# Attention of the running streams: from split matmuls over the whole array to plain float32 in four column strips

## The chip, the cores and the metric

The kernel runs on one core of a Trainium2 chip. The metric is the device time of one execution in microseconds, as the median of several executions. The kernel before takes 2970.55 us (median of 3, 2970.44 to 2970.97). One execution was taken by the hardware profiler; its own time and its records are what the profile shows.

The engines are TensorE (PE; loads of its stationary operand are listed apart as PEld), VectorE (DVE), ScalarE (ACT), GpSimd (POOL) and SyncE (SP), which here issues nearly all DMAs. Each engine takes its instructions in the order of its own queue.

## The reference, cut to what matters

The program is one inference step of a layer for two groups of requests: a prompt of 1040 positions (16 meta rows and 1024 frames) and eight running streams ("sample") with 16 new frames each. The change touches only the attention of the running streams. For each of the eight streams and 16 heads of width 64, 16 queries look at 272 cached keys and 16 new ones:

```
def stick_breaking(q, k, v, q_pos, k_pos):
    z = einsum('bqhd,bshd->bhqs', q, k) * (SB_HEAD_DIM ** -0.5)
    reach = k_pos[None, :] < q_pos[:, None]
    log_beta = log_sigmoid(z)
    log_keep = where(reach, log_sigmoid(-z), 0.0)
    later = cumsum(log_keep, axis=3, reverse=True) - log_keep
    w = where(reach, exp(log_beta + later), 0.0)
    return einsum('bhqs,bshd->bqhd', w, v)
```

So a weight is the sigmoid of its score times the product of one minus the sigmoids of all later keys. There is no softmax and no sum over rows. All inputs and outputs are float32.

## The kernel before, in words

The layer runs as phases in one program: norm and projections, the state-space part (`phase_ssd`), the prompt's attention (`phase_att`), the running streams' attention (`phase_smp`, which calls `sample_att`), the merge of the branches (`phase_merge`) and the feed-forward part. Big matmuls use a float32r form in which each operand is split into a high and a low part: `split` (L95 to L98) copies the rounded high part on ACT (L97) and subtracts it on DVE (L98), and `mm3` (L109 to L119) adds three products, high by high, high by low, low by high. `weights` (L100 to L107) loads and splits a weight tile in the same way.

`sample_att` works in 16 blocks: eight streams `b`, and in each two halves `hf` of eight heads, that is four pairs `j` of heads, 128 channels each. A block does this:

1. Load 256 cached keys and values of the half (`kt`, `vt`, L861 to L864, 512 KB each, on SP), from a common pool `ck` with four buffers.
2. Transpose the keys, eight 128x128 transposes into two `pk` tiles of PSUM (L135 is the line of every transpose), and split each into `Ksh` and `Ksl` (L97, L98). The last 16 cached keys and the 16 new keys are copied behind them by POOL (L869); the last 16 cached keys of all streams were transposed and split once ahead of the loop (`kch`, `kcl`).
3. Copy the queries, split as well, into `qdh` and `qdl` (L873): for pair `j` a stationary operand of 128 columns in which only columns 32j to 32j+31 are not zero, 16 for each head of the pair.
4. Scores `z`: four pairs times three products accumulate into one PSUM tile of 128 x 288 (L889, L892, L893). As each pair's operand is zero outside its own 32 columns, the sum over pairs puts pair `j` into rows 32j to 32j+31.
5. Weights: sigmoid on ACT (L895), the causal mask of the new keys and one minus it on POOL (L896, L898), a reversed running product on DVE (L899), and two multiplications on DVE (L902, L903).
6. Three transposes of the weights into `wT`, split into `wTh` and `wTl`. The values are split into `Vsh` (ACT, L882) and `Vsl` (POOL and DVE, L884). The last 32 values of four streams share tiles `V3h`, `V3l`, and `w3` holds the weights that belong to them, zero elsewhere.
7. Outputs `o`: three groups of keys times three products, 512 columns each (L912 to L914). Every row of the result holds its own weights against the values of all eight heads; only the diagonal blocks are wanted.
8. Copy the whole 128x512 to `od` (ACT, L916), transpose it in four pieces, and pick the diagonal blocks by two strided copies into `aout` (L924).

Between these blocks the gate projections run as filler. `paced` (L976 to L982) hands out three column tiles of a projection at a time; each is tied by `issue_after` to the first score matmul of a block (`marks`), so it cannot be issued earlier. Of the eight projections left after the prompt's attention six go into this phase, and RESERVE = 2 are kept for the start of the merge. All else about the order is set by a planner that simulates the program and orders each engine's queue by it (`schedule_with_timeline_sim`). A PSUM tile of the phase takes a whole bank: two for the gates, two `pk`, one `z`, two `wT`, one `o`. Pools of SBUF are laid out one behind the other in the order in which `phase_smp` names them, and a tile waits for the earlier users of its memory.

The merge begins with the two reserve gates, while `ssd_operands` (L941 on) loads rows of `s_y` into `yt` (L949), scales them (L951) and splits them (L952, L953).

`sample_state` (L528 on), in the state-space part, already writes plain float32 matmuls into 32-row slices of a PSUM tile (L549).

Of the kernel before, what the change touches and what calls it, by code (L numbers as in the profile page):

```python
# [13 lines left out]
F32 = mybir.dt.float32  # L14
F32R = mybir.dt.float32r
# [8 lines left out]
TP = META + SEQ  # L24
# [53 lines left out]
class Kernel:  # L78
# [738 lines left out]
    def sample_att(self, rate):  # L817
        nc, a, ap, pa = self.nc, self.a, self.ap, self.pa
        marks, done = [], 0
        out = self.tile(ap, [128, 8, TS], F32, 'aout', bufs=1)  # L820
        qs = [self.tile(ap, [128, 8, TS], F32R, n, bufs=1) for n in ('qhs', 'qls')]
        for t, src in zip(qs, (self.s_qh, self.s_ql)):
            nc.sync.dma_start(t.bitcast(F32), src[:, TP - T0:T2].rearrange("(j p) t -> p j t", p=128))

        kc, kn = ([self.tile(ap, [128, 8, TS], F32R, n + x, bufs=1) for x in 'hl'] for n in ('kc', 'kn'))
        for t, src in zip(kn, (self.s_kh, self.s_kl)):
            nc.sync.dma_start(t.bitcast(F32), src[:, TP:T].rearrange("(j p) t -> p j t", p=128))
        for hf in range(2):
            lk = self.tile(ap, [128, 512], F32, 'last', bufs=2)
            nc.sync.dma_start(lk, self.s_ck[:, 512 * hf:512 * hf + 512])  # L830
            pk = self.tile(pa, [128, 512], F32, 'pk', bufs=2)
            for j in range(4):
                self.T_(pk[:, 128 * j:128 * j + 128], lk[:, 128 * j:128 * j + 128])
            self.split(*(t[:, 4 * hf:4 * hf + 4] for t in kc), pk.rearrange("p (j s) -> p j s", j=4))
        qd = [[self.tile(ap, [128, 640], F32R, f'qd{x}{i}', bufs=1) for x in 'hl'] for i in range(2)]
        for i in range(2):
            for x in range(2):
                nc.gpsimd.memset(qd[i][x].bitcast(F32), 0.0)

        w3 = [self.tile(ap, [128, 224], F32, f'w3{hf}', bufs=1) for hf in range(2)]  # L840
        for x in w3:
            nc.gpsimd.memset(x, 0.0)
        for b in range(NB):
            if b % 4 == 0:
                V3 = []
                for hf in range(2):
                    c0 = 512 * hf
                    lv = self.tile(ap, [128, 512], F32, 'last', bufs=2)
                    for i in range(4):
                        cv = a['cache_v'][0, b + i].rearrange("s h d -> s (h d)")  # L850
                        nc.sync.dma_start(lv[32 * i:32 * i + 16], cv[256:272, c0:c0 + 512])
                        t0 = TP + 16 * (b + i)
                        nc.sync.dma_start(lv[32 * i + 16:32 * i + 32].rearrange("t (j c) -> t j c", c=128),
                                          self.s_v[4 * hf:4 * hf + 4, t0:t0 + 16].rearrange("j t c -> t j c"))
                    V3.append([self.tile(ap, [128, 512], F32R, n, bufs=2) for n in ('V3h', 'V3l')])
                    self.split(*V3[hf], lv)
            for hf in range(2):
# [5 lines left out]
                vt = self.tile(self.ckp, [128, 2, 512], F32, 'ck')  # L863
                nc.sync.dma_start(vt, cv[0:256].rearrange("(j p) c -> p j c", p=128))  # L864
                Kh, Kl = (self.tile(ap, [128, 4, 288], F32R, n) for n in ('Ksh', 'Ksl'))
                Q = qd[(2 * b + hf) % 2]
                for x, K in enumerate((Kh, Kl)):
                    for i, k in enumerate((kc, kn)):
                        nc.gpsimd.tensor_copy(K[:, :, 256 + 16 * i:272 + 16 * i],  # L869
                                              k[x][:, 4 * hf:4 * hf + 4, 16 * b:16 * b + 16].bitcast(F32))  # L870
                    for e in range(2):
                        es = slice(64 * e, 64 * e + 64)
                        nc.gpsimd.tensor_copy(Q[x].rearrange("p (j c) -> p j c", c=160)[es, :, 16 * e:16 * e + 16],  # L873
                                              qs[x][es, 4 * hf:4 * hf + 4, 16 * b:16 * b + 16].bitcast(F32))
                for j in range(0, 4, 2):
# [4 lines left out]
                    self.split(Kh[:, j:j + 2, 0:256], Kl[:, j:j + 2, 0:256], pk.rearrange("p (j c) -> p j c", j=2))  # L880
                Vh, Vl = (self.tile(ap, [128, 2, 512], F32R, n) for n in ('Vsh', 'Vsl'))
                nc.scalar.copy(Vh, vt)  # L882
                for i, eng in enumerate((nc.gpsimd, nc.vector)):
                    eng.tensor_tensor(out=Vl[:, i], in0=vt[:, i], in1=Vh[:, i].bitcast(F32), op=ALU.subtract)  # L884
                ps = self.tile(pa, [128, 512], F32, 'z')
                z = ps[:, 0:288]
                for j in range(4):
                    qh, ql = (Q[x][:, 128 * j:128 * j + 128] for x in range(2))
                    mk = nc.tensor.matmul(z, qh, Kh[:, j], start=(j == 0), stop=False)  # L889
                    if j == 0:  # L890
                        marks.append(mk)
                    nc.tensor.matmul(z, qh, Kl[:, j], start=False, stop=False)  # L892
                    nc.tensor.matmul(z, ql, Kh[:, j], start=False, stop=(j == 3))  # L893
# [10 lines left out]
                pt = self.tile(pa, [128, 512], F32, 'wT', bufs=2)  # L904
                for i, x in enumerate((B[:, 0:128], B[:, 128:256], w)):
                    self.T_(pt[:, 128 * i:128 * i + 128], x)
                wh, wl = (self.tile(ap, [128, 3, 128], F32R, n) for n in ('wTh', 'wTl'))
                self.split(wh, wl, pt[:, 0:384].rearrange("p (i c) -> p i c", c=128))
                po = self.tile(pa, [128, 512], F32, 'o')
                vs = [(Vh[:, 0], Vl[:, 0]), (Vh[:, 1], Vl[:, 1]), V3[hf]]  # L910
                for i, (vh, vl) in enumerate(vs):
                    nc.tensor.matmul(po, wh[:, i], vh, start=(i == 0), stop=False)  # L912
                    nc.tensor.matmul(po, wh[:, i], vl, start=False, stop=False)
                    nc.tensor.matmul(po, wl[:, i], vh, start=False, stop=(i == 2))  # L914
# [385 lines left out]
```

## Time and profile before

| what | value |
|---|---|
| median of 3 executions | 2970.55 us (2970.44 to 2970.97) |
| the profiled execution | 2969.59 us |
| its span, first to last instruction | 2967.9 us |
| mean granted TensorE clock | 0.994 |
| TensorE busy | 2909.5 us, 98% |
| first and last score matmul of the running streams (L889, L893) | 1481.5 and 1638.8 us |
| last transposes of `od` | from 1654.4 us |

In the profile a matmul's record runs from its start until its result has landed, so records of matmuls in sequence overlap, and busy time is not occupancy. The distance between starts of matmuls that follow each other without a wait is what one costs. In the views, a row of a timeline has start, duration, engine, line, operation, out<-in, the shape and a count of merged records; in brackets stands the idle time of the engine before it and what ended it. A row of groups has the shape and count, then busy time, mean ns of one, and idle time ahead. A row of a window gives its length and each engine's busy time and instructions, then the granted clock, the DMA engines' busy share and GB/s. A row of waits has total time, times and the longest.

### The profile page before, as it was taken

What the parts mean: (1) busy time and instruction counts of PE and PEld (TensorE: products, weight loads), DVE (VectorE), ACT (ScalarE), POOL (GpSimd) and SP (SyncE); (2) the same over time, 40 slices, a digit from 0 to 9 for tenths busy, and PEclk for the clock granted to TensorE, in tenths of its full rate; (3) what the DMA queues carried; (4) which work ended last, traced back from release to release, by engine and by line L of the source; (5) the groups of instructions that cost most, each with busy time, mean ns of one, the idle gap of its engine ahead of it and who ended that gap; (6) DMA issues with size and microseconds to landing.
All of it is one profiled execution on the core that took longest, in us unless ns stands there. A gap on an engine that the chain in (4) does not pass through costs nothing.

```text
span 2967.9 us, 45503 instructions
## 1 busy us (share of the span) xinstructions
PE 2909.5 (98%) x17399; PEld 2764.3 (93%) x17399; DVE 1711.7 (58%) x2578; ACT 1259.3 (42%) x2611; POOL 626.7 (21%) x1009
## 2 busy tenths in 40 slices
PE   7999999999999999999999999999999999999998
PEld 6998988989889999999899899999999999999998
DVE  6457666676657777777634531446655454545447
ACT  5445454454444455544544310224534242424245
POOL 1024132231322233333333000003201010101013
PEclk9999999999999999999999999999999999999999
DMA  6435355354574555554344642545211111111113
GB/s 196 115 86 159 110 150 149 88 158 118 155 224 136 138 139 145 147 139 106 110 155 132 203 152 87 166 122 170 60 48 44 44 44 37 45 44 44 37 44 121
DMA packets 430826, 338.98 MB, mean 114 GB/s; under 512 B 27264, under 2 KB 406476, under 8 KB 430600
## 3 DMA queue, kind: packets, MB, share of 16 engines
q1 hardware_dynamic: 429103, 333.25, 39.1%
q8 instruction: 137, 2.24, 0.3%
q10 hardware_dynamic: 1504, 2.82, 0.3%
q14 instruction: 82, 0.66, 0.1%
HBM read 244.84 MB, written 91.67 MB: 113 GB/s over the span
## 4 chain that ended last, share of the span: by engine, by line
PE 84%; DMA 5%; DVE 3%; ACT 2%; issue 1%; POOL 1%; SPq 1%; DVEq 0%; ACTq 0%; POOLq 0%
PE mm L115 23%; PE mm L118 22%; PE mm L119 22%; PE wT L135 2%; DMA yt<-s_y 1%; PE yd L501 1%; PE z L732 1%; PE z L735 1%; PE st L484 1%; PE px L135 1%; PE o L759 1%; DMA zf<-s_z 1%; PE o L756 1%; PE yo L510 1%; DMA wf<-in_w_out 1%
## 5 line engine op out<-in xcount | busy, mean ns | idle before, releaser
L115 PE MATMUL mm<-sh,wh 128*128 128x384 f32 (+3 forms) x2520 | 869.2, 346 | 5.0 <-ACT sh L952 1.8
L118 PE MATMUL mm<-sl,wh 128*128 128x384 f32 (+3 forms) x2520 | 868.8, 345 | 3.4 <-DVE sl L98 2.6
L119 PE MATMUL mm<-sh,wl 128*128 128x384 f32 (+3 forms) x2520 | 864.3, 343 | 0.0
L118 PEld LDWEIGHTS mm<-sl,wh 128*128 128x128 f32 (+1 forms) x2520 | 474.9, 188 | 18.7 <-issue 10.3
L115 PEld LDWEIGHTS mm<-sh,wh 128*128 128x128 f32 (+1 forms) x2520 | 474.6, 188 | 16.3 <-issue 5.2
L119 PEld LDWEIGHTS mm<-sh,wl 128*128 128x128 f32 (+1 forms) x2520 | 474.8, 188 | 9.2 <-issue 7.5
L106 DVE TENSOR_TENSOR wl<-wf,wh 128x1024 fp32r<-128x1024 f32 (+2 forms) x205 | 253.3, 1236 | 305.8 <-ACT wh L105 304.7
L118 PE MATMUL mm<-pl,wh 128*128 128x386 f32 x1248 | 424.9, 340 | 0.0
L115 PE MATMUL mm<-ph,wh 128*128 128x386 f32 x1248 | 424.6, 340 | 0.0
L119 PE MATMUL mm<-ph,wl 128*128 128x386 f32 x1248 | 422.8, 339 | 1.2 <-DVE wl L106 1.1
L105 ACT CAST wh<-wf 128x1024 fp32r<-128x1024 f32 (+2 forms) x205 | 212.7, 1038 | 478.3 <-PE mm L118 455.9
L1167 DVE SCALAR_TENSOR_TENSOR acc<-fx,cwf,acc 128x384 f32<-128x384 f32 (+1 forms) x352 | 170.9, 516 | 155.4 <-ACT acc L1165 151.7
L119 PEld LDWEIGHTS mm<-ph,wl 128*128 128x128 f32 x1248 | 236.2, 189 | 2.3 <-DVE wl L106 1.8
L115 PEld LDWEIGHTS mm<-ph,wh 128*128 128x128 f32 x1248 | 236.3, 189 | 0.6
L118 PEld LDWEIGHTS mm<-pl,wh 128*128 128x128 f32 x1248 | 235.2, 188 | 1.7
L699 DVE TENSOR_TENSOR_SCAN keep<-keep 128x144 f32<-128x144 f32 (+7 forms) x128 | 180.1, 1409 | 52.0 <-POOL keep L698 51.3
L115 PE MATMUL mm<-ah,wh 128*128 128x384 f32 x528 | 179.7, 340 | 0.0
L119 PE MATMUL mm<-ah,wl 128*128 128x384 f32 x528 | 179.2, 339 | 0.0
L118 PE MATMUL mm<-al,wh 128*128 128x384 f32 x528 | 178.9, 339 | 0.0
L1094 POOL TENSOR_TENSOR sq<-sq,sq 128x386 f32<-128x386 f32 (+1 forms) x39 | 57.9, 1484 | 446.4 <-ACT sq L1093 438.5
L1192 DVE TENSOR_TENSOR h<-mm,h 128x384 f32<-128x384 f32 x144 | 79.7, 555 | 120.0 <-PE mm L119 119.5
L98 DVE TENSOR_TENSOR wTl<-wT,wTh 128x512 fp32r<-128x512 f32 (+3 forms) x176 | 102.9, 602 | 77.1 <-ACT wTh L97 76.4
(334 smaller groups left out, 4526.0 us busy)
## 6 DMA issues: line engine op xcount, KB each, us to landing
wf<-in_w_in SPq DMA_DIRECT2D x80, 512.0 KB
wf<-in_w_up SPq DMA_DIRECT2D x44, 512.0 KB
t<-s_ac SPq DMA_DIRECT2D x36, 512.0 KB
wf<-in_w_down SPq DMA_DIRECT2D x28, 512.0 KB
wf<-in_w_out SPq DMA_DIRECT2D x24, 512.0 KB
s_y<-x SPq DMA_DIRECT2D x16, 577.0 KB
yt<-s_y SPq DMA_DIRECT2D x16, 577.0 KB
KH<-s_kh SPq DMA_DIRECT2D x32, 260.0 KB
```

The source lines that it names most:

```text
L98: nc.vector.tensor_tensor(out=l, in0=x, in1=h.bitcast(F32), op=ALU.subtract)
L105: nc.scalar.copy(wh, wf)
L106: nc.vector.tensor_tensor(out=wl, in0=wf, in1=wh.bitcast(F32), op=ALU.subtract)
L115: i = nc.tensor.matmul(p, wh[:, k, :], mh[:, c:c + w], start=s, stop=False)
L118: nc.tensor.matmul(p, wh[:, k, :], ml[:, c:c + w], start=False, stop=False)
L119: nc.tensor.matmul(p, wl[:, k, :], mh[:, c:c + w], start=False, stop=e)
L135: self.nc.tensor.transpose(out, in_, self.ident[:k, :k])
L484: first = nc.tensor.matmul(pS, Bt, xe.rearrange("p h d -> p (h d)"), start=True, stop=True)
L699: nc.vector.tensor_tensor_scan(out=K[:, ::-1], data0=K[:, ::-1], data1=K[:, ::-1], initial=1.0, op0=ALU.mult, op1=ALU.min)
L1094: nc.gpsimd.tensor_tensor(out=acc[:, :w], in0=acc[:, :w], in1=sq, op=ALU.add)
L1167: nc.vector.scalar_tensor_tensor(out=op, in0=src(q), scalar=w(q), in1=op, op0=ALU.mult, op1=ALU.add)
L1192: self.nc.vector.tensor_tensor(out=h, in0=p, in1=h, op=ALU.add)
```

## The change

The running streams' attention no longer splits anything. Queries and new keys are put together again from their stored parts (one addition each, DVE and POOL); cached keys, values and weights stay as they are. Each pair of heads gets its own strip of 32 columns of the array: the stationary operand of the scores is 128x32 in place of 128x128, four matmuls write four 32-row slices of `z`, each complete in itself. The outputs are twelve matmuls, three groups of keys for each strip, and each strip multiplies only with its own pair's 128 values, so the result is 128x128 and already holds just the wanted heads (and within a pair both heads' products). It needs one transpose in place of four, into the same bank. The two copies of transposed keys go one to ACT and one to DVE. `V3` is loaded straight into its tile. PSUM: `wT` goes from two banks to one, `o` from one to two. SBUF: `vt` gets its own pool with four buffers in the phase, so that `ck` serves keys alone. Pacing, RESERVE and all else stay. The line numbers below 815 don't change.

```diff
-        qs = [self.tile(ap, [128, 8, TS], F32R, n, bufs=1) for n in ('qhs', 'qls')]
-        for t, src in zip(qs, (self.s_qh, self.s_ql)):
-            nc.sync.dma_start(t.bitcast(F32), src[:, TP - T0:T2].rearrange("(j p) t -> p j t", p=128))
...
+        both = lambda n: [self.tile(ap, [128, 8, TS], F32, n + x, bufs=1) for x in 'hl']
+        qs, kn = both('q'), both('kn')
...
+        for (h, l), eng in ((qs, nc.vector), (kn, nc.gpsimd)):
+            eng.tensor_tensor(out=h, in0=h, in1=l, op=ALU.add)
+        q, kn = qs[0], kn[0]
+        kc = self.tile(ap, [128, 8, TS], F32, 'kc', bufs=1)
...
-            self.split(*(t[:, 4 * hf:4 * hf + 4] for t in kc), pk.rearrange("p (j s) -> p j s", j=4))
+            nc.scalar.copy(kc[:, 4 * hf:4 * hf + 4], pk.rearrange("p (j s) -> p j s", j=4))
+        qd = [self.tile(ap, [128, 4, 32], F32, f'qd{i}', bufs=1) for i in range(2)]
...
-                vt = self.tile(self.ckp, [128, 2, 512], F32, 'ck')
+                vt = self.tile(ap, [128, 2, 512], F32, 'vt', bufs=4)
...
-                    self.split(Kh[:, j:j + 2, 0:256], Kl[:, j:j + 2, 0:256], pk.rearrange("p (j c) -> p j c", j=2))
-                Vh, Vl = (self.tile(ap, [128, 2, 512], F32R, n) for n in ('Vsh', 'Vsl'))
-                nc.scalar.copy(Vh, vt)
-                for i, eng in enumerate((nc.gpsimd, nc.vector)):
-                    eng.tensor_tensor(out=Vl[:, i], in0=vt[:, i], in1=Vh[:, i].bitcast(F32), op=ALU.subtract)
+                    (nc.vector.tensor_copy if j else nc.scalar.copy)(K_[:, j:j + 2, 0:256], pk.rearrange("p (j c) -> p j c", j=2))
...
                 for j in range(4):
-                    qh, ql = (Q[x][:, 128 * j:128 * j + 128] for x in range(2))
-                    mk = nc.tensor.matmul(z, qh, Kh[:, j], start=(j == 0), stop=False)
+                    mk = nc.tensor.matmul(z[32 * j:32 * j + 32], Q[:, j], K_[:, j], start=True, stop=True)
                     if j == 0:
                         marks.append(mk)
-                    nc.tensor.matmul(z, qh, Kl[:, j], start=False, stop=False)
-                    nc.tensor.matmul(z, ql, Kh[:, j], start=False, stop=(j == 3))
...
-                pt = self.tile(pa, [128, 512], F32, 'wT', bufs=2)
+                pt = self.tile(pa, [128, 512], F32, 'wT')
...
-                wh, wl = (self.tile(ap, [128, 3, 128], F32R, n) for n in ('wTh', 'wTl'))
-                self.split(wh, wl, pt[:, 0:384].rearrange("p (i c) -> p i c", c=128))
-                po = self.tile(pa, [128, 512], F32, 'o')
-                vs = [(Vh[:, 0], Vl[:, 0]), (Vh[:, 1], Vl[:, 1]), V3[hf]]
-                for i, (vh, vl) in enumerate(vs):
-                    nc.tensor.matmul(po, wh[:, i], vh, start=(i == 0), stop=False)
-                    nc.tensor.matmul(po, wh[:, i], vl, start=False, stop=False)
-                    nc.tensor.matmul(po, wl[:, i], vh, start=False, stop=(i == 2))
-                od = self.tile(ap, [128, 512], F32, 'od', bufs=1)
-                nc.scalar.copy(od, po)
-                pd = self.tile(pa, [128, 512], F32, 'wT', bufs=2)
-                for j in range(4):
-                    self.T_(pd[:, 128 * j:128 * j + 128], od[:, 128 * j:128 * j + 128])
+                wt = self.tile(ap, [128, 3, 4, 32], F32, 'wt')
+                nc.scalar.copy(wt, pt[:, 0:384].rearrange("p (i j c) -> p i j c", i=3, j=4))
+                po = self.tile(pa, [128, 512], F32, 'o', bufs=2)
+                for i, v in enumerate((vt[:, 0], vt[:, 1], V3[hf])):
+                    for j in range(4):
+                        nc.tensor.matmul(po[32 * j:32 * j + 32, 0:128], wt[:, i, j], v[:, 128 * j:128 * j + 128],
+                                         start=(i == 0), stop=(i == 2))
+                od = self.tile(ap, [128, 128], F32, 'od')
+                nc.scalar.copy(od, po[:, 0:128])
+                self.T_(po[:, 128:256], od)
...
             self.ap = {n: self.pool(c2, "smpa_" + n, 2) for n in (
-                'last', 'qdh0', 'qdl0', 'qdh1', 'qdl1', 'qhs', 'qls', 'knh', 'knl', 'kch', 'kcl', 'Ksh', 'Ksl', 'V3h', 'V3l',
-                'v', 'r', 'newton', 'beta', 'keep', 'Vsh', 'Vsl', 'w30', 'w31', 'wTh', 'wTl', 'od', 'aout')}
+'last', 'qd0', 'qd1', 'w30', 'w31', 'qh', 'ql', 'knh', 'knl', 'kc', 'Ks', 'vt', 'v', 'r', 'newton', 'beta', 'keep',
+                'V3', 'wt', 'od', 'aout')}
```

More of the change, by code (lines that the diff above doesn't have):

```diff
@@ L833, in sample_att @@
                 self.T_(pk[:, 128 * j:128 * j + 128], lk[:, 128 * j:128 * j + 128])
[L834 to L838 removed]
+            nc.scalar.copy(kc[:, 4 * hf:4 * hf + 4], pk.rearrange("p (j s) -> p j s", j=4))
+        qd = [self.tile(ap, [128, 4, 32], F32, f'qd{i}', bufs=1) for i in range(2)]
         w3 = [self.tile(ap, [128, 224], F32, f'w3{hf}', bufs=1) for hf in range(2)]
[L841 removed]
+        for x in qd + w3:
             nc.gpsimd.memset(x, 0.0)
@@ L844, in sample_att @@
             if b % 4 == 0:
-                V3 = []
+                V3 = [self.tile(ap, [128, 512], F32, 'V3', bufs=4) for hf in range(2)]
                 for hf in range(2):
                     c0 = 512 * hf
-                    lv = self.tile(ap, [128, 512], F32, 'last', bufs=2)
                     for i in range(4):
                         cv = a['cache_v'][0, b + i].rearrange("s h d -> s (h d)")
-                        nc.sync.dma_start(lv[32 * i:32 * i + 16], cv[256:272, c0:c0 + 512])
+                        nc.sync.dma_start(V3[hf][32 * i:32 * i + 16], cv[256:272, c0:c0 + 512])
                         t0 = TP + 16 * (b + i)
-                        nc.sync.dma_start(lv[32 * i + 16:32 * i + 32].rearrange("t (j c) -> t j c", c=128),
+                        nc.sync.dma_start(V3[hf][32 * i + 16:32 * i + 32].rearrange("t (j c) -> t j c", c=128),
                                           self.s_v[4 * hf:4 * hf + 4, t0:t0 + 16].rearrange("j t c -> t j c"))
-                    V3.append([self.tile(ap, [128, 512], F32R, n, bufs=2) for n in ('V3h', 'V3l')])
-                    self.split(*V3[hf], lv)
             for hf in range(2):
@@ L862, in sample_att @@
                 nc.sync.dma_start(kt, ck[0:256].rearrange("(j p) c -> p j c", p=128))
-                vt = self.tile(self.ckp, [128, 2, 512], F32, 'ck')
+                vt = self.tile(ap, [128, 2, 512], F32, 'vt', bufs=4)
                 nc.sync.dma_start(vt, cv[0:256].rearrange("(j p) c -> p j c", p=128))
-                Kh, Kl = (self.tile(ap, [128, 4, 288], F32R, n) for n in ('Ksh', 'Ksl'))
+                K_ = self.tile(ap, [128, 4, 288], F32, 'Ks')
                 Q = qd[(2 * b + hf) % 2]
[L867 to L874, printed above, removed]
+                for i, k in enumerate((kc, kn)):
+                    nc.gpsimd.tensor_copy(K_[:, :, 256 + 16 * i:272 + 16 * i], k[:, 4 * hf:4 * hf + 4, 16 * b:16 * b + 16])
+                for e in range(2):
+                    es = slice(64 * e, 64 * e + 64)
+                    nc.gpsimd.tensor_copy(Q[es, :, 16 * e:16 * e + 16], q[es, 4 * hf:4 * hf + 4, 16 * b:16 * b + 16])
                 for j in range(0, 4, 2):
```

11 lines of the change are left out of this document (5 added, 6 removed).

## The prediction

> **What bounds the kernel now.** First the page, the line of busy times and that of what the DMAs moved in each fortieth of the span:
>
> ```profile
> PE 2909.5 (98%) x17399; PEld 2764.3 (93%) x17399; DVE 1711.7 (58%) x2578; ACT 1259.3 (42%) x2611; POOL 626.7 (21%) x1009
> ...
> GB/s 196 115 86 159 110 150 149 88 158 118 155 224 136 138 139 145 147 139 106 110 155 132 203 152 87 166 122 170 60 48 44 44 44 37 45 44 44 37 44 121
> ```
>
> TensorE is busy for 98% of the span, so work taken from it counts, if the stage that it is taken from is bound by it too. The edit lies in `sample_att`, whose instructions stand between 1472 and 1655 us. So, second, the windows over that stretch:
>
> ```profile
> core 0: us, PE busy (x) PEld busy (x) DVE busy (x) ACT busy (x) POOL busy (x), PEclk, DMA share, GB/s
> 1472.00:1482.00 10.00, 5.13 (x27) 4.09 (x28) 6.00 (x9) 5.82 (x9) 9.51 (x23) 0.73 0.55 154
> 1482.00:1500.00 18.00, 18.00 (x99) 17.93 (x98) 2.84 (x6) 3.88 (x8) 2.59 (x12) 0.87 0.44 144
> 1500.00:1540.00 40.00, 39.54 (x246) 37.32 (x245) 19.44 (x33) 17.54 (x37) 17.30 (x53) 1.00 0.49 157
> 1540.00:1580.00 40.00, 40.00 (x247) 38.17 (x247) 16.63 (x27) 19.53 (x39) 14.78 (x34) 1.00 0.42 128
> 1580.00:1620.00 40.00, 39.10 (x250) 37.48 (x249) 18.10 (x31) 18.63 (x39) 18.62 (x52) 1.00 0.54 163
> 1620.00:1657.00 37.00, 33.08 (x173) 27.68 (x172) 14.90 (x24) 17.66 (x35) 6.91 (x10) 0.91 0.42 126
> ```
>
> In the middle 120 us TensorE idles 0.46 + 0 + 0.90 = 1.4 us, every other engine at least half. Head (4.9 us idle, clock 0.73) and tail (3.9 us) are different: there latency rules. Third, which waits:
>
> ```profile
> PE pk L135 <- DVE kcl L98: 3.0, 1, 3.0
> PE wT L135 <- ACT od L916: 2.4, 3, 1.0
> ```
>
> The first is the start (the split of the last cache rows), the second the tail.
>
> Fourth, the gates that fill the stage, in its groups by form; with them what the change removes on other engines:
>
> ```profile
> L115 PE MATMUL mm<-sh,wh 128*128 128x384 f32 x99 | 34.8, 352 | 0.0
> L98 DVE TENSOR_TENSOR Ksl<-pk,Ksh 128x512 fp32r<-128x512 f32 x32 | 21.3, 685 | 9.7 <-ACT Ksh L97 9.7
> L115 PE MATMUL mm<-sh,wh 128*128 128x386 f32 x48 | 16.5, 344 | 0.0
> L884 POOL TENSOR_TENSOR Vsl<-ck,Vsh 128x512 fp32r<-128x512 f32 x16 | 26.5, 1661 | 66.3 <-ACT Vsh L882 66.2
> L106 DVE TENSOR_TENSOR wl<-wf,wh 128x1024 fp32r<-128x1024 f32 x6 | 7.4, 1226 | 8.1 <-ACT wh L105 8.1
> ```
>
> 99 + 48 less three that belong to the next phase are 144 triples: six gates of 24. They stay.
>
> **The change part by part.** A matmul's duration holds its latency; what it costs is the distance to the next start. From TensorE's timeline:
>
> ```profile
> 1526.92 0.40 PE L912 MATMUL o<-Vsh,wTh 128*128 128x512 f32 x1
> ...
> 1528.31 0.29 PE L889 MATMUL z<-Ksh,qdh 128*128 128x288 f32 x1
> ...
> 1529.77 0.30 PE L893 MATMUL z<-Ksh,qdl 128*128 128x288 f32 x1
> 1529.90 0.60 PE L135 MATMUL pk<-ident,ck 128*128 128x128 f32 x4
> 1530.34 0.60 PE L135 MATMUL wT<-ident,od 128*128 128x128 f32 x4
> ...
> 1540.28 0.34 PE L118 MATMUL mm<-sl,wh 128*128 128x384 f32 x1
> ...
> 1543.80 0.34 PE L115 MATMUL mm<-sh,wh 128*128 128x386 f32 x1
> ```
>
> *Removed, per block (there are 16).* Twelve score matmuls: 1528.31 to 1529.90 = 1.59 us. Nine output matmuls: six in 1526.92 to 1528.31, 0.232 each, 2.09 us. Of the transposes of `od` (four at 0.11, as in 1529.90 to 1530.34) three go, one stays. With all four: 1.59 + 2.09 + 0.44 = 4.12 us.
>
> *Added.* Four plain float32 matmuls of 288 columns and twelve of 128, each into 32 of the array's columns, and one transpose. The kernel has this form already, in `sample_state`:
>
> ```profile
> L549 PE MATMUL ms<-hT,bc 128*32 128x128 f32 x256 | 16.0, 285 | 0.0
> L563 PE MATMUL ms<-bm,xes 128*128 128x512 f32 x32 | 16.8, 606 | 0.0
> ```
>
> L549 is written 128 times and recorded 256 times, so plain float32 is two passes. From 128 to 512 columns a pass grows by 606 - 285 = 321 ns, 0.836 ns a column: 0.107 us for 128, 0.24 us for 288. Do strips run side by side?
>
> ```profile
> 222.31 0.34 PE L115 MATMUL mm<-sh,wh 128*128 128x384 f32 x1
> 222.48 0.33 PE L118 MATMUL mm<-sl,wh 128*128 128x384 f32 x1
> 222.75 0.42 PE L549 MATMUL ms<-hT,bc 128*32 128x128 f32 x8
> 223.10 0.66 PE L135 MATMUL px<-ident,t 128*128 128x128 f32 x4
> 223.69 1.09 PE L501 MATMUL yd<-t,xd 128*64 128x128 f32 x16
> ```
>
> Eight records of 285 ns lie within 0.42 us; in a row they would take 8 x 0.107 = 0.86 before the last one's latency. So four strips take the time of one. The gate's matmuls start 0.176 apart (twenty in 1540.28 to 1543.80), so the strips could have begun at 222.66; the next operation begins at 223.10. Of these 0.44 us two passes are 0.21; 0.23 is the price of entering and leaving strips. The four transposes behind take 0.59 instead of 0.44, a part of it the next change of form, so the price lies between 0.23 and 0.38. I take 0.25.
>
> Scores: 2 x 0.24 + 0.25 = 0.73. Outputs: 3 groups x 2 x 0.107 + 0.25 = 0.89. One transpose 0.11. Together 1.73 against 4.12: 2.39 a block, **38.2 us** in 16. With 0.38 a switch it is 34. Strips of 288 columns, and twelve in a row, the trace doesn't show; with no overlap at all scores cost 1.92 + 0.25 and outputs 12 x 2 x 0.107 + 0.25 = 2.82, 5.1 in all, and the 16 blocks lose 16 us. The row of four side by side is the nearest; I take full overlap.
>
> The Trainium skill, "TensorEngine Tiling (Array Packing)", section Key Properties, speaks against it: a change of tiling mode drains TensorE. That is the 0.23 us. "TensorE: Matmul & The Clock Gate", section Measured speedup vs the span model, gives three column strips a speedup of 2.38 rather than 3; an estimate by that ratio (3.2 for four) puts 1.12 us of streaming at 1.4 us and the gain at about 34 us. Here eight records within 0.42 us speak for fuller overlap.
>
> *Scores torn.* `K_` comes in two halves, one copied by ACT, one by DVE (0.59 and at most the 0.685 of `Ksl`). If two strips start before the other two are ready, a block pays a second pass pair or switch, 0.25 to 0.7. I take half the blocks at 0.25: **-2** (0 to -11).
>
> *Other engines.* Per block the splits of K and V go: two of 0.685 and one more on DVE, 1.66 on POOL, about 1.6 on ACT, also the 128x512 copy of `od`. None was the bound, so that gives nothing directly. What it does is shorten latencies.
>
> *Cover lost.* In the chain of a block TensorE must do something else while the others work:
>
> ```profile
> 1638.79 0.30 PE L893 MATMUL z<-Ksh,qdl 128*128 128x288 f32 x1
> ...
> 1639.17 0.41 ACT L895 ACTIVATE beta<-z 128x288 f32<-128x288 f32 x1 [1.53 <-issue]
> ...
> 1640.45 0.76 DVE L899 TENSOR_TENSOR_SCAN keep<-keep 128x288 f32<-128x288 f32 x1 [1.35 <-POOL keep L898]
> ...
> 1643.36 0.50 PE L912 MATMUL o<-Vsh,wTh 128*128 128x512 f32 x1 [0.69 <-ACT wTh L97]
> ...
> 1653.04 0.63 PE L914 MATMUL o<-V3h,wTl 128*128 128x512 f32 x1
> ...
> 1654.81 0.42 PE L115 MATMUL mm<-sh,wh 128*128 128x384 f32 x1
> ```
>
> From the sigmoid to the end of the scan 1639.17 to 1641.21 is 2.0 us; with two multiplications, the copies and hops it is about 4 us a block. Today's cover is the gates, 432 x 0.176 / 16 = 4.8 us a block, and the other blocks' matmuls; of these 2.39 us go. If the order of the queue stays, waits can eat between nothing and all 38.2 us of it. TensorE takes its queue in order: behind outputs that wait for the copied weights stand the next block's transposes and the gates, and ACT, DVE and POOL wait for these. Since the gates alone exceed the chain, but stand in clumps (1540 to 1544 holds nothing else), I take a fifth: **-7.5**.
>
> *Tail.* From the last scores (1638.79) to the first reserve gate (1654.81) are 16.0 us. Eighteen of its output matmuls run 0.43 apart instead of 0.232 and wait three times. Its 23 output matmuls and 14 transposes are 6.9 us at full rate, so 9 are lost. After the change the last block needs 2.7 us to its weights, 0.33 + 0.5 for transposes and copy, 0.9 for outputs, about 0.8 for copy and transpose, some 6 to 7 us, 2.7 of it work: about 4 lost. I take **+4** (0 to +6).
>
> *Head.* Scores cannot start before `q`, the sum of two loads, and its copy into the strips' layout:
>
> ```profile
> 1470.57 0.57 SPq L823 DMA_DIRECT2D qhs<-s_qh  x1
> ```
>
> Today one half is loaded at 1470.57, as its memory comes free late. In the new order of pools both lie where that memory comes free, the four V buffers too; then an addition of 128x1024 on DVE (as L106, 1.2 us) and on POOL twice the 1.66 of L884 at most. Against that go the two splits of 1.3 us and the 2 us of `Vsh` ahead of them. **-1** (-6 to +2). DMAs stay in number; at 128 to 163 GB/s in the middle windows they would need about 145 x 182.5 / 150 = 176 in a shorter stage, and the page shows up to 224.
>
> *The next phase.* Its operands are loaded as memory of this stage comes free:
>
> ```profile
> L949 SPq DMA_DIRECT2D yt<-s_y x16: 319/320/383, 1639.0 to 1720.9; - x16
> PE mm L115 <- ACT sh L952: 1.8, 2, 1.1
> ```
>
> The first loads go 16 us before the stage ends, when the query tiles are free. Afterwards that memory belongs to tiles used until the last transposes of the weights, so the loads begin some 10 us nearer to the end. Two reserve gates (2 x 12.7 us) cover them; today 1.8 us are waited. **-1** (-4 to +1).
>
> **Sum:** 38.2 - 2 - 7.5 + 4 - 1 - 1 = 30.7 us. The profiled execution took 2969.59 us (span 2967.9 and 1.7 around it), so 2938.9; the median shown is 0.96 above it: 2939.9, **2940 us**.
>
> **Rivals.** *Waits take the place of the work* (2948 to 2963): the order keeps its clumps, half or more of the removed 38.2 comes back as waits of TensorE on ACT's copies; 30.7 - 12 to 30.7 - 23 remain. For it: the chain of 4 us; against: 4.8 us of gates a block. *More than the sum* (about 2930): covers hold, scores aren't torn: 38.2 + 4 less 2 = 40. For it: only 1.4 us idle in the middle today. *The clock falls* (about 2970): idle stretches are followed by half speed, as the 0.73 and 0.87 at the head show. Work left in the stage is 76 + 16 x (1.73 + 11 x 0.11) = 123 us; if a quarter of it runs at half speed, 31 us are gone. The Trainium skill, "TensorE: Matmul & The Clock Gate", section on the HAM clock gate, has half rate after one idle window of about 3.4 us; by that rule, gaps under 2 us in mid-stage would not trip it. *Slower: strips torn apart.* The scheduler sets other work between strips; each then pays its own passes and switch: scores 4 x 0.73 = 2.9, outputs 12 x (0.21 + 0.25) = 5.5, 8.5 a block against 4.12, 70 us slower, 3041. It decides from about 38.2 / 16 / 0.25 = 9.5 extra switches a block. Against it: the eight of L549 are together in the trace, and all twelve outputs wait for one copy.
>
> **How the numbers follow.** Forecast (2932 to 2948) 0.58; waits 0.22; more 0.11; clock 0.05; slower 0.04. The range 2926 to 2958 holds the forecast, two thirds of the waits and most of "more". What can be told from no change is 0.2%, 6 us: faster 0.92 (the first three, and a little of the clock), same 0.03, slower 0.05.
>
> **What would show it.** Scores as 128 records and outputs as 384, 128x32, in bunches of 8 and 24 that start close together; the stretch between 1472 and the first reserve gate near 150 us instead of 182.5. If a bunch of 24 takes over 1.2 us, the overlap is wrong; if TensorE idles over 12 us in the middle, the cover is; if the clock there is under 0.95, the gate is. It is wrong as a whole if the stage takes over 170 us.

## The result, and the profile after

The changed kernel takes **2933.4 us** (median of four runs, 2932.05 to 2936.45) against 2970.49 us for the kernel before, measured beside it (2967.62 to 2970.97). The ratio is 0.9875, 95% interval 0.9863 to 0.9887: 37 us faster. A second copy of the same kernel, timed later beside other runs of the kernel before (2967.95), came to 2934.03 us, ratio 0.9888 (0.9873 to 0.9903): 34 us. The forecast was 2940, range 2926 to 2958.

The profiled execution took 2936.45 us, its span is 2934.7, so 33.2 less than the span before. First the line of busy times of its page, then the windows over the stage (columns as in the prediction):

```profile
PE 2873.4 (98%) x17527; PEld 2712.9 (92%) x17527; DVE 1677.3 (57%) x2525; ACT 1228.9 (42%) x2575; POOL 588.3 (20%) x928
```

```profile
1472.00:1482.00 10.00, 4.82 (x29) 2.82 (x28) 4.11 (x9) 2.69 (x4) 3.83 (x8) 0.77 0.68 190
...
1500.00:1540.00 40.00, 39.78 (x337) 33.54 (x338) 10.09 (x21) 13.41 (x33) 7.97 (x27) 1.00 0.54 170
1540.00:1580.00 40.00, 40.00 (x324) 33.03 (x323) 11.31 (x21) 13.08 (x34) 7.63 (x30) 1.00 0.57 179
1580.00:1620.00 40.00, 35.35 (x327) 26.45 (x327) 12.19 (x22) 16.70 (x42) 6.07 (x22) 0.97 0.53 160
```

The picture is the old one, shifted: TensorE busy for 98% of a shorter span, in mid-stage idle for 0.22 us of 80 at full clock, DVE, ACT and POOL less busy. The last window now holds the tail.

Where the stage begins and ends is read from TensorE's timeline. Before, the first transposes of the last cached keys and the first scores:

```profile
1472.46 1.07 PE L135 MATMUL pk<-ident,last 128*128 128x128 f32 x8
1481.47 0.61 PE L889 MATMUL z<-Ksh,qdh 128*128 128x288 f32 x1 [1.34 <-POOL Ksh L869]
```

and after, the same two, with the first reserve gate that ends the stage:

```profile
1470.02 1.07 PE L135 MATMUL pk<-ident,last 128*128 128x128 f32 x8
...
1481.25 1.19 PE L880 MATMUL z<-Ks,qd 128*32 128x288 f32 x8
...
1618.62 0.67 PE L115 MATMUL mm<-sh,wh 128*128 128x384 f32 x1
```

From 1472.46 to 1654.81 were 182.3 us; from 1470.02 to 1618.62 are **148.6**. The stage is 33.7 us shorter. What lies ahead of the stage is the same code and came 2.4 us earlier here; what follows, to the first matmul of the merge's own projection, took 2.9 us longer.

Now the bunches of strips, in the same timeline:

```profile
1494.68 0.64 PE L901 MATMUL o<-vt,wt 128*32 128x128 f32 x16
1495.14 0.40 PE L901 MATMUL o<-V,wt 128*32 128x128 f32 x8
1495.47 0.44 PE L119 MATMUL mm<-sh,wl 128*128 128x386 f32 x1
1495.75 0.34 PE L115 MATMUL mm<-sh,wh 128*128 128x386 f32 x1
...
1497.43 0.69 PE L880 MATMUL z<-Ks,qd 128*32 128x288 f32 x8
1498.05 0.88 PE L135 MATMUL pk<-ident,ck 128*128 128x128 f32 x6
...
1517.46 0.68 PE L880 MATMUL z<-Ks,qd 128*32 128x288 f32 x4 [0.22 <-POOL qd L870]
1518.07 0.65 PE L135 MATMUL pk<-ident,ck 128*128 128x128 f32 x4
1518.66 0.68 PE L880 MATMUL z<-Ks,qd 128*32 128x288 f32 x4
...
1520.29 0.68 PE L880 MATMUL z<-Ks,qd 128*32 128x288 f32 x4
1520.90 0.44 PE L115 MATMUL mm<-sh,wh 128*128 128x384 f32 x1
1521.18 0.34 PE L118 MATMUL mm<-sl,wh 128*128 128x384 f32 x1
```

Twenty-four output records run from 1494.68 to 1495.47, 0.79 us, and the gate matmul behind them takes 0.28 to the next in place of 0.176: 0.89 us in all, the forecast's figure. Eight score records take 0.62 (1497.43 to 1498.05), and a gate behind scores again 0.28 (1520.90 to 1521.18), 0.10 too much: 0.72 in all, where 0.73 was forecast. But from 1517.46 on the scores come as four and four, with transposes between, and **four records take as long as eight** (0.61). Two passes of two strips last as long as two passes of four; a bunch torn in two pays everything twice. Through the stage ten of the sixteen blocks are torn by other work like this, and three more run as two and two right behind each other.

The groups by form over the whole stage (busy time, mean ns of one, idle ahead) have the numbers of records that were forecast, 128 and 384:

```profile
L880 PE MATMUL z<-Ks,qd 128*32 128x288 f32 x128 | 19.6, 433 | 0.7 <-DVE Ks L876 0.4 <-POOL qd L870 0.2
L901 PE MATMUL o<-vt,wt 128*32 128x128 f32 x256 | 10.8, 280 | 0.7 <-ACT wt L897 0.6
L901 PE MATMUL o<-V,wt 128*32 128x128 f32 x128 | 6.9, 282 | 0.0
```

Last, the waits of TensorE in the stage (total, times, longest):

```profile
PE pk L135 <- DVE Ks L876: 3.5, 2, 3.3
PE o L135 <- ACT od L904: 2.7, 2, 2.2
PE mm L115 <- ACT sh L937: 2.0, 1, 2.0
```

The longest of each is at the head, in the tail and in the merge; from 1500 us to the last blocks there is none over 0.41 us. The head in the timeline of TensorE and DVE:

```profile
1474.87 1.23 DVE L828 TENSOR_TENSOR qh<-qh,ql 128x1024 f32<-128x1024 f32 x1 [3.37 <-DMA ql<-s_ql]
1476.01 0.68 DVE L876 COPY Ks<-pk 128x512 f32<-128x512 f32 x1
...
1476.76 0.66 PE L135 MATMUL pk<-ident,ck 128*128 128x128 f32 x4 [3.32 <-DVE Ks L876]
```

DVE's first copy of keys stands in its queue behind the addition of the queries, which waits for the load of `ql`; TensorE waits 3.32 us for that copy. And the tail, in the chain of waits (start, length, what):

```profile
1609.46 5.75 DMA wf<-in_w_out
...
1615.29 0.04 ACT wh L105
...
1616.24 0.26 ACT od L904
```

The copy of a finished output, `od`, stands on ACT behind the cast of a weight tile of the next phase, and that waits for its load.

### The profile page after: what moved, and what is told of

It is laid out like the page before. It is cut to its first block, busy times and chain, and to the rows that moved or that the text cites. A ratio compares the mean times of both kernels' runs of the same rounds, so it can differ in the third digit from the quotient of the medians.

```text
span 2934.7 us, 45551 instructions
## 1 busy us (share of the span) xinstructions
PE 2873.4 (98%) x17527; PEld 2712.9 (92%) x17527; DVE 1677.3 (57%) x2525; ACT 1228.9 (42%) x2575; POOL 588.3 (20%) x928
## 4 chain that ended last, share of the span: by engine, by line
PE 83%; DMA 7%; DVE 3%; ACT 2%; issue 1%; SPq 1%; POOL 0%; DVEq 0%; ACTq 0%; POOLq 0%
PE mm L115 22%; PE mm L118 22%; PE mm L119 22%; PE wT L135 2%; PE yd L501 1%; PE z L732 1%; PE z L735 1%; DMA zf<-s_z 1%; PE st L484 1%; PE o L759 1%; PE px L135 1%; DMA yt<-s_y 1%; PE o L756 1%; DMA wf<-in_w_out 1%; PE yo L510 1%
## 5 line engine op out<-in xcount | busy, mean ns | idle before, releaser
L118 PEld LDWEIGHTS mm<-sl,wh 128*128 128x128 f32 (+1 forms) x2520 | 473.9, 188 | 19.0 <-issue 10.5
L119 PEld LDWEIGHTS mm<-sh,wl 128*128 128x128 f32 (+1 forms) x2520 | 474.0, 188 | 10.5 <-issue 9.1
L1146 POOL COPY cs<-fx 128x2 f32<-128x2 f32 x44 | 42.5, 965 | 465.7 <-ACT fx L1138 465.7
```

Source lines behind the costliest of these rows:

```text
L118: nc.tensor.matmul(p, wh[:, k, :], ml[:, c:c + w], start=False, stop=False)
L119: nc.tensor.matmul(p, wl[:, k, :], mh[:, c:c + w], start=False, stop=e)
L1146: nc.gpsimd.tensor_copy(cs[:, e, 0:2], x[:, n0 - 2:n0])
```

## The experiments

Each kernel's profile was divided in the same way. All times are us; z and o are the distances from each score or output matmul's start to the next start on TensorE, summed over the 16 blocks, with the waits that fall between them; tail is from the last scores to the end of the stage; merge is from there to its own projection. The stage starts with the first transposes; a wait of TensorE just ahead of them is not in it (1.9, 2.2 and 2.1 us in *early*, *early5* and *tail*, none in the others). The runs were made in groups, each beside the kernel before, whose median was 2967.3 to 2970.5 us; between groups the ratios compare better than the medians.

| kernel | median | ratio to before, interval | stage | to first scores | z | o | idle in stage | tail | merge |
|---|---|---|---|---|---|---|---|---|---|
| before | 2970.5 | 1 | 182.3 | 9.0 | 28.8 | 40.6 | 10.1 | 16.0 | 332.8 |
| after | 2933.4 | 0.9863 to 0.9887 | 148.6 | 11.2 | 18.2 | 13.5 | 10.4 | 8.1 | 335.7 |
| again | 2934.0 | 0.9873 to 0.9903 | 147.7 | 11.3 | 18.2 | 13.7 | 9.5 | 7.8 | 334.1 |
| whole | 2972.2 | 1.0006 to 1.0025 | 188.1 | 9.7 | 30.1 | 38.6 | 8.7 | 10.1 | 333.1 |
| outputs | 2941.2 | 0.9899 to 0.9929 | 157.8 | 5.3 | 31.9 | 14.3 | 11.5 | 5.7 | 333.6 |
| scores | 2964.8 | 0.9980 to 0.9999 | 181.0 | 10.1 | 16.4 | 44.6 | 15.0 | 23.0 | 334.4 |
| together | 2930.6 | 0.9862 to 0.9891 | 142.5 | 11.4 | 10.4 | 14.4 | 11.1 | 8.0 | 335.5 |
| order | 2933.3 | 0.9868 to 0.9897 | 147.5 | 6.8 | 19.6 | 13.4 | 8.8 | 8.0 | 331.1 |
| both | 2927.7 | 0.9846 to 0.9879 | 140.1 | 7.2 | 10.5 | 14.2 | 9.7 | 7.8 | 334.8 |
| reserve5 | 2929.2 | 0.9859 to 0.9888 | 107.6 | 11.2 | 10.8 | 14.3 | 12.9 | 12.1 | 368.5 |
| reserve8 | 2931.2 | 0.9857 to 0.9887 | 70.5 | 10.8 | 18.3 | 14.4 | 12.7 | 7.3 | 406.0 |
| early | 2926.5 | 0.9842 to 0.9875 | 136.4 | 4.4 | 10.0 | 14.3 | 6.0 | 7.9 | 335.8 |
| early5 | 2931.7 | 0.9864 to 0.9893 | 106.0 | 4.7 | 10.9 | 14.1 | 11.0 | 9.3 | 369.7 |
| tail | 2923.8 | 0.9833 to 0.9866 | 134.8 | 4.4 | 10.1 | 13.8 | 5.5 | 6.1 | 334.8 |

### Is it the strips? The whole array, and each half of the change alone

*whole*: the changed kernel, plain float32 and without splits, but with operands of 128 columns, zero outside a pair's own, and four transposes of the outputs, as before the change (the matmuls of its edit, shortened).

```diff
-mk = nc.tensor.matmul(z[32 * j:32 * j + 32], Q[:, j], K_[:, j], start=True, stop=True)
+mk = nc.tensor.matmul(z, Q[:, 128 * j:128 * j + 128], K_[:, j], start=(j == 0), stop=(j == 3))
...
-for j in range(4):
-    nc.tensor.matmul(po[32 * j:32 * j + 32, 0:128], wt[:, i, j], v[:, 128 * j:128 * j + 128], ...)
+nc.tensor.matmul(po, wt[:, i], v, start=(i == 0), stop=(i == 2))
```

> The changed kernel without strips: queries, keys, values and weights stay unsplit float32, but the stationary operands are 128 columns wide again with zeros outside a pair's 32, four score matmuls of 288 columns and three output matmuls of 512 accumulate over the whole array, and four transposes pick the diagonal. Theory 'strips': plain float32 takes two passes at 0.836 ns a column, so scores are 8 x 0.24 = 1.9 and outputs 6 x 0.427 = 2.6 us a block, with the transposes 4.9 against 2.2 measured in the changed kernel: 44 us more, 2977 us (2970 to 2984), no faster than the kernel before. Rival 'the splits': what was gained came from the splits that ACT, DVE and POOL no longer make, so most of it stays: 2935 to 2950.

Measured 2972.2 us, ratio 1.0016, as the theory of the strips has it. Leaving the splits out gives nothing by itself. In the timeline of *whole* the scores of a block:

```profile
1530.13 2.11 PE L880 MATMUL z<-Ks,qd 128*128 128x288 f32 x8
1532.07 1.04 PE L135 MATMUL pk<-ident,ck 128*128 128x128 f32 x8
```

Eight passes in a row take 1.94 us, one 0.24, where the three products of the kernel before took 1.59 (1528.31 to 1529.90, shown ahead of the result); over the whole array plain float32 is thus a fifth dearer. In strips the bunch of eight takes 0.62: its first four records start within 0.02 us, the other four 0.27 later, so the four strips overlap fully. A quarter of 1.94 is 0.49, and what is left of 0.72, 0.23, goes to getting in and out. The Trainium skill, "TensorEngine Tiling (Array Packing)", section Key Properties, says that a change of tiling mode drains TensorE. The trace agrees in that going in and out costs something here, 0.23 to 0.25 us a bunch; a drain as such it does not show.

*outputs*: the kernel before, with only the outputs in strips (scores still split). *scores*: the kernel before, with only the scores in strips (values and weights still split). The lines of the strips in the two edits, shortened:

```diff
...
+wt = self.tile(ap, [128, 3, 4, 32], F32, 'wt')
+        nc.tensor.matmul(po[32 * j:32 * j + 32, 0:128], wt[:, i, j], v[:, 128 * j:128 * j + 128], ...)
...
+    mk = nc.tensor.matmul(z[32 * j:32 * j + 32], Q[:, j], K_[:, j], start=True, stop=True)
```

> The kernel before with the change's part for weights, values and outputs alone; queries, keys and scores are split as before. Theory 'strips': outputs and the transposes behind them fall from 47.6 us (40.6 and 7.0 between their starts and the next) to about 16.6, so 31 us, less what returns as waits: 2940 us (2935 to 2945). Rival 'the splits of K are what ACT and DVE were late with': under half of the gain, over 2950.

> The kernel before with the change's part for queries, keys and scores alone; values and weights are split as before and outputs use the whole array. Theory 'strips': scores fall from 28.8 us to 18.2 if as many blocks are torn, to 10.4 if none: 2957 us (2948 to 2962). Rival 'the splits of K are what ACT and DVE were late with': over half of the gain, under 2950.

*outputs* came to 2941.2, 26 us faster, as expected. *scores* came to 2964.8, 2.5 us faster than the 2967.3 of the kernel before measured beside it, and outside its range (2948 to 2962). Its score matmuls did save 12.4 us (28.8 to 16.4). Its waits and a window of it show where these went:

```profile
PE wT L135 <- ACT od L911: 2.8, 4, 1.0
PE o L909 <- DVE wTl L98: 2.3, 1, 2.3
```

```profile
1620.00:1657.00 37.00, 29.67 (x136) 22.79 (x135) 13.85 (x20) 15.73 (x31) 4.35 (x6) 0.77 0.51 149
```

Most of it went into the tail, which grew from 16 to 23 us. Three blocks' outputs are left over at the end, as before the change (27 and 25 of 144 output matmuls), and wait for the split of their weights and the copies of their results; but TensorE idles 7.3 us there in place of 3.9, and the clock of the window from 1620 to 1657 is 0.77 in place of 0.91. Why the same leftover waits longer is not shown. So the two halves are worth 2.5 and 26 alone and 34 together. By the tails (23.0 with *scores*, 5.7 with *outputs*, 8.1 with both) the 5 us between lie at the end, which the outputs in strips shorten and the scores in strips alone lengthen. Strips of split operands were not run, so what strips would give without plain float32 stays open.

### Torn bunches

*together*: each strip of the scores is ordered behind the one before it, and the two that wait for the later copy (DVE's) go first, so that all four start only when all keys are there.

```diff
-for j in range(4):
-    mk = nc.tensor.matmul(z[32 * j:32 * j + 32], Q[:, j], K_[:, j], start=True, stop=True)
+for j in (2, 3, 0, 1):
+    prev, mk = mk, nc.tensor.matmul(z[32 * j:32 * j + 32], Q[:, j], K_[:, j], start=True, stop=True)
+    if prev is not None:
+        self.issue_after(mk, prev)
```

> The changed kernel, but the four score matmuls of a block are issued one behind the other, those of the later copied half of the keys first, and the pace mark is the last of them. Theory 'tearing': in the changed kernel ten of the 16 blocks have their four strips in two pieces with other work between, and half a bunch takes TensorE as long as a whole one (0.61 against 0.62 us to the next start), so the scores cost 18.2 us where 16 bunches would cost about 10. Joined, 6 us go: 2927 us (2925 to 2929), scores near 0.65 us a block. Rival 'the tears lie where TensorE would wait anyway': the time stays at 2933 (2931 to 2935), and the waits of TensorE on the key copies grow by what the scores lose.

*again* is the changed kernel itself, beside it:

> The changed kernel unaltered, for comparison in the same batch. Expected 2933 us, ratio 0.9875 to the kernel before; all theories agree.

The group of the scores in *together*:

```profile
L881 PE MATMUL z<-Ks,qd 128*32 128x288 f32 x128 | 12.4, 432 | 1.7 <-DVE Ks L876 1.1 <-POOL beta L887 0.4
```

The same 128 records are busy for 12.4 us in place of 19.6. From start to start the scores fall from 18.2 to 10.4, 0.65 a block. The stage is 5.2 us shorter than in *again*, the time 3.4 (2930.6 and 2934.0, ranges that meet at 2933.3), which lies between the two forecasts. So tearing is shown, and the rival is right in part: of the 7.8 us that the scores lose, about 2 come back as short waits for the keys in mid-stage (TensorE's idle time there goes from 0.7 to 2.6 us).

### The head

*order*: in the list of SBUF pools `Ks` moves to where memory comes free late, so that queries and new keys lie in memory that comes free earlier: `qh` is loaded at 1443 us in place of 1468.

```diff
-'last', 'qd0', 'qd1', 'w30', 'w31', 'qh', 'ql', 'knh', 'knl', 'kc', 'Ks', 'vt', 'v', 'r', 'newton', ...
+'last', 'Ks', 'qd0', 'qd1', 'w30', 'w31', 'knh', 'knl', 'qh', 'ql', 'kc', 'vt', 'v', 'r', 'newton', ...
```

> The changed kernel, only the pools of the phase in another order: the key tiles Ks stand where the memory comes free last, the loads of queries and new keys lie in memory that the head before last frees. Theory 'head': the first score matmul waits for the loads of queries and for what DVE, POOL and ACT do behind them (in the changed kernel it starts 11.2 us after the phase's first transposes, before the change 9.1), so it starts 3 to 6 us after the first key transposes instead; and the next phase's first operand loads, which take over the memory of the first pools, start earlier before the phase's end. 2933 - 4 - 1 = 2928 us (2925 to 2931). Rival 'the head is bound by something else' (the square root's table load ahead of ACT's key copies, the two buffers for transposed keys, the late cold clock): 2931 to 2935, the first scores still about 9 to 11 us after the first transposes.

> Scores joined and pools reordered together. If both theories hold, the gains add up: 2922 us (2919 to 2926). If the tears lie in waits anyway and the head is bound elsewhere, 2933. If only one holds, 2927 or 2928.

The first scores came 6.8 us after the first transposes in place of 11.3, yet the stage and the time (2933.3, the rival's) stayed. The timeline of *order*:

```profile
1474.39 1.28 ACT L920 ACT_TABLE_LOAD   x1 [2.63 <-DMA v<-s_ss]
...
1476.68 1.07 ACT L838 COPY kc<-pk 128x512 f32<-128x512 f32 x2
...
1477.32 1.97 PE L135 MATMUL pk<-ident,ck 128*128 128x128 f32 x8 [3.85 <-ACT kc L838]
```

DVE's wait is gone, and ACT has taken its place: its copies of the last keys stand behind the root of another part (L920, `norm_rows`), which waits for the load of `v`: one of the things that the rival named. When the first scores start is thus no measure of what the head costs; TensorE does other work ahead of them, and its idle time up to there fell only from 5.2 us in *again* to 3.9. *both* is *order* and *together* in one: 2927.7, where 2922 was expected if the gains add and 2927 or 2928 if one alone holds.

*early*: as *both*, with the tiles of that root, `v`, `r`, `newton`, first in the list, so that the load lies ahead of all.

```diff
-'last', 'qd0', 'qd1', 'w30', 'w31', 'qh', 'ql', 'knh', 'knl', 'kc', 'Ks', 'vt', 'v', 'r', 'newton', ...
+'v', 'r', 'newton', 'last', 'Ks', 'qd0', 'qd1', 'w30', 'w31', 'knh', 'knl', 'qh', 'ql', 'kc', 'vt', ...
```

> Scores' strips one behind the other as in together, and in the list of SBUF pools v, r and newton come first, then last and Ks, so that the load v<-s_ss of norm_rows and its square root on ACT lie ahead of the copies of the last keys. Theory (after the order was changed, ACT's copies of kc queued behind the table load of that square root, 3.3 to 3.9 us): the wait pk <- kc goes from 3.3 to under 1 us, the stage from 140 to about 136.5 us, the time to about 2924 us (2921 to 2926). Rival (the first loads of keys and their transposes set the head anyway, or the tile last now waits longer for its memory): the wait only changes its name, 2926 to 2930 us as in both (2927.7).

The stage fell to the expected 136.4 us, the first scores to 4.4 us after the start. But a part of that is only the start moved. Of TensorE's waits, the one at the head:

```profile
PE pk L135 <- DMA last<-s_ck: 1.9, 1, 1.9
```

ACT's copies are no longer waited for, but TensorE now waits 1.9 us for the load of the last keys, just ahead of the first transposes and so outside the stage as it is counted. That load is issued at 1468.5 us; in *both* it was at 1295.5. With the wait the stage is 138.2 us, 1.9 less than in *both* and not 3.7: half of the old wait is gone, half has changed its name, as the rival said. The median fell by 1.2 us (2926.5 against 2927.7, ranges 2924.8 to 2927.6 and 2924.9 to 2931.5), which these runs do not tell from nothing.

### Cover: fewer gates, none

The forecast took 7.5 us off for cover lost. *reserve5* leaves three gates in the phase in place of six, *reserve8* none; the rest waits for the merge. *early5* is *early* with three.

```diff
-RESERVE = 2
+RESERVE = 5    (reserve8: 8)
```

> The changed kernel with five of the eight last gate projections kept for the next phase and three in this one, in place of two and six: the same matmuls, half the cover. Theory 'cover' (the prediction's term for lost cover): about 4 us a block of ACT, POOL and DVE work stand between a block's scores and its outputs; with 2.4 us of gates a block 1.6 and more come bare, and TensorE idles 20 to 30 us more in the phase: 2950 to 2960 us. Rival 'the planner lays the blocks side by side': several blocks are under way at once and cover each other, the idle time of the phase stays within 5 us of the changed kernel's 10, and the longer lead of the next phase saves some of its waits for operands: 2928 to 2936.

> The changed kernel with RESERVE = 8: no gate in the phase at all, all eight at the merge's start. TensorE's own work in the stage is then about 148 - 81 - 10 = 57 us in 16 blocks, 3.6 us a block, less than the chain of about 4 us from sigmoid to weights. Theory of cover (it decides once less than the chain is left): TensorE idles 25 to 40 us in the stage, stage 85 to 100 us, the time 2940 to 2960 us. Rival (the planner lays two or three blocks side by side, and their work covers each other): idle as in reserve5 (13 us), stage about 70 us, the time 2925 to 2932 us; the loads, 16.8 MB, would then have to come at about 240 GB/s, which the stretch of 1500 to 1520 us of reserve5 shows (278). A middle course, bound by the loads at 200 GB/s: stage 85 to 90, 2940 us.

> As early, with RESERVE = 5: three gates in the phase, five at the merge's start. If what reserve5 gained (4.8 us against the same kernel with two) and what early gains are in different places they add: about 5 us below early, 2919 us (2915 to 2923). If both only remove the same wait: within 2 us of early. If with three gates the head's late start is felt more: above early.

*reserve5* came to 2929.2 us and *reserve8* to 2931.2, both as the rival had it. With no gate at all the stage takes 70.5 us and TensorE idles 12.7 us in it, 2.3 more than in the changed kernel, over half of it at the head as there. The windows of *reserve8*, and a stretch of its timeline:

```profile
1470.00:1490.00 20.00, 12.42 (x82) 6.63 (x82) 9.29 (x20) 6.32 (x11) 9.57 (x29) 0.57 0.71 236
1490.00:1510.00 20.00, 17.91 (x232) 11.43 (x230) 9.79 (x20) 11.70 (x33) 6.97 (x29) 1.00 0.79 273
1510.00:1530.00 20.00, 20.00 (x301) 13.22 (x299) 13.34 (x27) 13.94 (x41) 9.06 (x36) 1.00 0.89 319
```

```profile
1493.81 0.68 PE L880 MATMUL z<-Ks,qd 128*32 128x288 f32 x4
...
1496.82 0.69 PE L880 MATMUL z<-Ks,qd 128*32 128x288 f32 x8
...
1497.33 0.42 DVE L892 TENSOR_TENSOR beta<-beta,keep 128x256 f32<-128x256 f32 x1
...
1498.14 0.64 PE L901 MATMUL o<-vt,wt 128*32 128x128 f32 x16
...
1499.42 0.38 PE L135 MATMUL wT<-ident,beta 128*128 128x128 f32 x2
...
1499.84 0.69 PE L880 MATMUL z<-Ks,qd 128*32 128x288 f32 x8
1500.15 0.48 ACT L897 COPY wt<-wT 128x384 f32<-128x384 f32 x1
...
1501.16 0.64 PE L901 MATMUL o<-vt,wt 128*32 128x128 f32 x16
```

A block takes 3.0 us here. The block whose last scores start at 1493.81 has its weights worked out on DVE from 1497.33, transposed at 1499.42, copied at 1500.15, and its outputs at 1501.16, 7.4 us after the scores. That is longer than the chain of 4 us, because TensorE meanwhile does the scores of the next two blocks (1496.82, 1499.84) and the outputs of an earlier one (1498.14). **The blocks cover each other**, and up to 319 GB/s the loads keep up but for one wait of 2.1 us. The cover theory falls.

Why did *reserve5* gain 4.8 us on *again*, and *reserve8* only 2.8? Not by more than chance: the two have the same ratio to the kernel before (0.9873 and 0.9872), and from the start of the stage to the merge's own projection they take 476.1 and 476.5 us, *again* 481.9. What they gain fits the bunches: with fewer gates the planner's order happened to tear only one block of 16 in *reserve5* and two in *reserve8*. (That the scores of *reserve8* still add up to 18.3 us comes from 5.1 us of waits between them and from the slow clock at the head.) That reading says that *early5* cannot gain from it, as nothing is torn in *early*, and it did not: 2931.7, 5 us above *early*, while 2919 was expected of gains that add. The longest of its waits in total:

```profile
PE pk L135 <- DMA ck<-in_cache_k: 3.6, 3, 2.1
```

In a stage of 106 us the keys come late three times, in *early* never. That accounts for 3.6 us; from the stage to the merge's own projection the two profiles differ by 3.8.

### The tail

*tail*: as *early*, with the copies of weights and outputs on DVE.

```diff
-nc.scalar.copy(wt, pt[:, 0:384].rearrange("p (i j c) -> p i j c", i=3, j=4))
+nc.vector.tensor_copy(wt, pt[:, 0:384].rearrange("p (i j c) -> p i j c", i=3, j=4))
-nc.scalar.copy(od, po[:, 0:128])
+nc.vector.tensor_copy(od, po[:, 0:128])
```

> As early, with the copies of the weights (wt) and of the outputs (od) moved from ACT to DVE. Theory (the last blocks' copies stand on ACT behind casts of w_out tiles that wait for their load; in early 1.6 us before 1606.4): in the last stretch TensorE's wait for od falls from 2.1 us to under 0.7, the time from last scores to the first reserve gate from 7.9 to about 6 us, the time to about 2924.5 us (2922 to 2926). Rival (DVE's queue has the subtractions of the same w_out tiles, wl, which wait for the same load; or the tail's saving is given back as a wait for the next phase's scaled rows): no gain, 2926 to 2928 us.

Measured 2923.8 us (2923.5 to 2925.4), ratio 0.985, 2.7 us below *early*; the ranges overlap by 0.6 us. Its timeline:

```profile
1605.81 1.05 ACT L105 CAST wh<-wf 128x1024 fp32r<-128x1024 f32 x1 [1.25 <-DMA wf<-in_w_out]
...
1605.96 0.33 PE L135 MATMUL o<-ident,od 128*128 128x128 f32 x1 [0.41 <-DVE od L906]
```

ACT still waits for the weight tile, now alone. The longest wait for `od` is 0.41 us, the tail 6.1 us as expected. This is the fastest version here, 10 us below the changed kernel.

## Why the prediction was right, and where it was not

The direction and the size hold: 30.7 us were summed, the spans differ by 33.2 and the medians by 34 and 37. By its steps:

- **Strips, 38.2**: right, and each price in it. 0.72 and 0.89 us a block were measured for the 0.73 and 0.89 reckoned, and the switch is about the 0.25 that was taken. The Trainium skill, "TensorE: Matmul & The Clock Gate", section Measured speedup vs the span model, gives three column strips 2.38 rather than 3. The wary estimate by that ratio was not needed: the overlap of four is full here.
- **Scores torn, -2**: the mechanism was right, its size wrong. At 0.73 a block 16 blocks are 11.7 us; 18.2 were measured, **-6.5** or somewhat more (*together* took 7.8 out of the scores, of which 5.2 reached the stage). Ten blocks were torn, not eight, and a torn block pays a second whole bunch, 0.61, not 0.25. The step named "a second pass pair or switch, 0.25 to 0.7"; it took the cheap end, though with only two strips ready the passes of those two must be paid in full.
- **Cover lost, -7.5**: wrong, the step that failed. Measured about **0**: 0.22 us idle from 1500 to 1580, and 2.3 us more in a stage without any gate. The step weighed the chain of 4 us against the gates, named the other blocks' matmuls but did not count on them, and put the outputs in their way; it did not see that the next blocks' keys and scores need nothing of this block's weights, so that the planner can put them between.
- **Tail, +4**: right. From 16.0 to 8.1 us, of which the last block's work is 2.7: 5.4 lost in place of 9, **+3.6** (+3.3 if one counts the 25 output matmuls that the trace has there; the step took 23). It was reckoned at 6 to 7; the rest is the weight tile of the next phase, which the step did not see and *tail* took away.
- **Head, -1**: right. The first scores come 11.2 us after the start in place of 9.0, but TensorE's idle time ahead of them rose only from 4.9 to 5.5 us, **-0.7**. The reason is the one named (the addition of the queries), but by way of DVE's queue: the copy of keys stood behind the addition.
- **Next phase, -1**: the merge took 335.7 us in place of 332.8. Other profiles with two reserve gates show 331.1 to 335.8, so -2.9 can't be told from nothing.

So two errors of about 4.5 and 7.5 us of opposite sign cancelled in good part; that the sum came so near is to that extent luck. Of the rivals, "more than the sum" described the middle rightly (the covers hold) and the scores wrongly (they were torn); "waits take the place", "the clock falls" (1.00 from 1500 to 1580) and "torn apart" as a loss are out for this kernel. *scores* shows that the first of them is a real course of things: there 12.4 us of matmuls were saved and 2.5 us of time.

## What to carry to other kernels

Price strips as the passes of one strip plus one switch, and for that price see to it that all of a bunch are ready together, by an explicit order of issue: half a bunch costs as much as a whole one. Before taking off for lost cover, ask whether the next tile's first steps need anything of this tile's last ones. When a stage gets shorter, look at each engine's queue at its two ends: a small copy behind something that waits for a load was the price in the head and in the tail, and it moved from one engine to the other, and at the head in part to another load, when the order was changed; in the tail it went when the copy stood elsewhere.

## What was not expected of the hardware

Plain float32 over the whole array takes 1.94 us for a block's scores, three products of split operands 1.59. Yet *whole*, without any split and with less work on DVE, ACT and POOL, is within 0.3% of the kernel before. Without strips nothing of the gain is left.

An idle start goes with a slow clock and so seems to be paid twice. In *reserve8* TensorE was busy for 12.42 of the 20 us from 1470 on, and the clock granted there was 0.57; from 1490 on it was 1.00.

The part of the program ahead of the stage, whose code no edit touches, ended between 1466.6 and 1474.6 us in the profiles of these kernels. A single profile can't show a gain of a few microseconds by its span; the stage's own length does.
